# Weight tiles moved by 64 bytes inside their SBUF partition

## The chip, the cores and the metric

The kernel runs on one core of a Trainium2 chip. The metric is the device time of one execution in microseconds (us); the time quoted for a kernel is the median of its runs. Engines are named as in the profile: PE is TensorE's matmul side, PEld its weight loads, DVE is VectorE, ACT is ScalarE, POOL is GpSimd, SP is the engine whose queue issues the DMAs.

## The reference

The reference computes one batch of 256 tokens of width 1024 through two blocks, all in fp32.

The first block is a mixer (8 heads of causal attention with a learned decay, beside a depthwise convolution of width 31), a cross attention over 256 memory tokens, and a mixture of experts: 32 experts in 4 groups, one group and two experts of it for each token. The second block has two layers. Each is a gated feed-forward network (1024 to 2816 to 1024), a mixing part (a gated linear recurrence in layer 0, stick-breaking attention of 16 heads in layer 1) and a second feed-forward network:

```
y = (silu(t @ w_gate[e]) * (t @ w_up[e])) @ w_down[e]         # expert e, 1024 -> 512 -> 1024
x = x + 0.5 * ((silu(h @ w_g) * (h @ w_u)) @ w2)              # feed-forward, four of them
x = x + rglru(...)          # layer 0
x = x + stick_breaking(...) # layer 1
```

All weights, about 400 MB, are read once from HBM.

## The kernel before, in words

**Layout.** Activations lie with channels on the 128 partitions and the 256 tokens along the free dimension. A weight is brought in tiles of 128 partitions x 2048 fp32 values (8192 bytes of each partition, 1 MB in all).

**Three matmuls for one.** Outside the experts each fp32 product is made of three matmuls on values rounded to fp32r. `wload` (L136 to L160) brings a tile to `raw`; ACT rounds it into `wh` (L157), DVE writes the rest, `raw - wh`, into `wl` (L158). Activations are split in the same way into a high and a low part by `split`: `xgh`/`xgl` for a normed input, `hh`/`hl` for a feed-forward network's middle. `mm3` (L174) then issues, for each 128 x 128 piece of weight,

```
mm(out, w[0], x[0], start=first, stop=False)   # wh with the high part
mm(out, w[0], x[1], start=False, stop=False)   # wh with the low part
mm(out, w[1], x[0], start=False, stop=last)    # wl with the high part
```

The weight is the operand that is loaded into the array (a PEld row of the profile, 128 columns), and the activation is streamed through it (a PE row, 256 columns). The next weight load runs while the matmul before it streams. `proj2` runs 48 such matmuls over a tile into one PSUM tile, with `xgh`/`xgl` as streams; `rowproj` runs 48 over a tile of the down projection, with `hh`/`hl` (in the recurrence `yh`/`yl`, in the cross attention `cath`/`catl`) as streams. In `product` (values, keys and queries) the roles are exchanged: activations are loaded and weight tiles are streamed, 512 columns at a time.

**A feed-forward network** has 11 rounds; each runs 48 matmuls for the gate, 48 for the up projection, and, in rounds two to ten, the 48 of the down projection of the round before. So PE's order in a round is 96 matmuls with `xg` streams and 48 with `hh`/`hl` streams. The last two down projections run together at the end, 96 matmuls (528 down matmuls for each of the four networks).

**The experts** run on plain fp32 tiles, streamed straight from where the DMA put them (L941, L967). A ring of 16 places holds them: the 8 buffers of `raw`, 3 of `wh`, 3 of `wl`, and the two tiles `xgh` and `xgl`, which are free in that stage. SP issues the next load (L171) when PE has used a place's old content.

**Memory.** Pools lie one behind the other in each partition, tiles in the order of their first use, each rounded up to 32 bytes: constants first, then `weights` (`raw`, `wh`, `wl`), then `temps` (small work tiles; the last of them is `nr16`, 6 buffers of 64 bytes), then `xgh` and `xgl`, then the pools of the stages. Where a tile begins, in bytes past a multiple of 128:

| tile | role outside the experts | before |
|---|---|---|
| `raw`, `wh`, `wl` | weights | 32 |
| `xgh`, `xgl`; `yh`, `yl` of the recurrence; `catl`; the mixer's four | streams | 64 |
| `hh`, `hl`; `xkvh`, `xkvl` | streams | 96 |
| `cath` of the cross attention | stream | 32 |
| `oh`, `oT` of the experts' routing | streams | 0 |
| `tokh`, `tokl` (tokens, loaded as weights by L846) | loaded | 96 |

Pieces of a tile begin a multiple of 512 bytes (weights) or 1024 bytes (streams) behind its start, so all pieces of a tile have the tile's own offset. `rsqrt` makes four work tiles of the tag `nr{n}`; with `n` = 16 it is called from `head_norm` alone, with one more tile of that tag live, and `after_moe` holds one such tile earlier on.

Of the kernel before, what the change touches and what calls it, by code (L numbers as in the profile page):

```python
# [10 lines left out]
I32 = mybir.dt.int32  # L11
# [5 lines left out]
P = 128  # L17
T = 256
D = 1024
KC = D // P  # L20
# [22 lines left out]
def bc(ap, shape, at):  # L43

    return ap.unsqueeze(at).to_broadcast(shape)


class Block:
    def __init__(s, ctx, tc, io):
        s.tc, s.nc, s.ctx, s.io = tc, tc.nc, ctx, io  # L50
        s.n = s.turn = s.place = 0
        s.queue = None
        pool = lambda name, bufs, **k: ctx.enter_context(tc.tile_pool(name=name, bufs=bufs, **k))
        s.cp = pool("const", 1)
        s.wp = pool("weights", 3)
        s.tp = pool("temps", 2)
        s.xp = pool("x", 1)
        s.pa = pool("acc", 1, space=PSUM)
        s.pp = pool("ps", 2, space=PSUM)
# [165 lines left out]
    def rsqrt(s, x, n):  # L225

        nc = s.nc
        xh = s.tmp([P, n], f"nr{n}", 6 if n > 4 else 8)
        nc.vector.tensor_scalar_mul(xh, x, -0.5)
        yi = s.tmp([P, n], f"nr{n}", 6 if n > 4 else 8).bitcast(I32)  # L230
        nc.vector.tensor_single_scalar(yi, x.bitcast(I32), 1, op=ALU.arith_shift_right)
        y = s.tmp([P, n], f"nr{n}", 6 if n > 4 else 8)
        nc.vector.tensor_scalar(y.bitcast(I32), yi, -1.0, float(0x5F3759DF), op0=ALU.mult, op1=ALU.add)
        u = s.tmp([P, n], f"nr{n}", 6 if n > 4 else 8)
        for _ in range(3):
            if n == 2:
                for i in range(n):
                    c = slice(i, i + 1)
                    nc.vector.scalar_tensor_tensor(u[:, c], y[:, c], xh[:, c], y[:, c], op0=ALU.mult, op1=ALU.mult)
            else:  # L240
                nc.vector.tensor_mul(u, y, y)
                nc.vector.tensor_mul(u, u, xh)
            nc.vector.scalar_tensor_tensor(y, u, 1.5, y, op0=ALU.add, op1=ALU.mult)
        return y
# [61 lines left out]
    def rows(s, st, n=D, tag="acc3"):  # L306


        got = {}

        def rows(what):
            if not got:
                got["pb"], a = s.bank(tag)
                got["x"], got["y"] = s.rstd(s.colsum(st, a[:, 0:2]), n)
            if what not in got:
                got[what] = s.spread(got["y"], got["pb"])
            return got[what]
        return rows
# [705 lines left out]
    def after_moe(s, acc, p2):  # L1024


        nc = s.nc
        gg = s.new(p2, [P, KC], "gg")
        nc.vector.tensor_mul(gg, s.col("final_g", 0, 8), s.col("ffn1_norm_2", 0, 8))

        g2 = s.tmp([P, 2 * KC], "nr16", 6).rearrange("p (k n) -> p k n", n=2)
        nc.vector.memset(g2, 1.0)
        nc.vector.tensor_mul(g2[:, :, 1], s.col("final_g", 0, 8), s.col("final_g", 0, 8))
        xg = s.pair(s.xp, KC, "xg")
        st = s.sums_pe(g2)
        for b in range(4):
            s.update(acc[b], b, 1.0, xg, gg, st)
        got = {}

        def rows(what):  # L1040
            if not got:


                x = s.tmp([P, 4], "nr4", 8)
                pb = s.bank()[0]
                nc.vector.tensor_scalar_mul(x.rearrange("p (n h) -> p n h", h=2), st["pe"].rearrange("p h n -> p n h"), 1.0 / D)
                nc.vector.tensor_scalar_add(x[:, 0:2], x[:, 0:2], EPS)
                nc.vector.scalar_tensor_tensor(x[:, 2:4], x[:, 0:2], EPS, x[:, 2:4], op0=ALU.mult, op1=ALU.add)
                y = s.rsqrt(x, 4)
                got["r"] = s.spread(y[:, 2:4], pb)  # L1050
                got["r1"] = s.spread(y[:, 0:2], pb, s.tmp([P, T]))
            return got[what]

        def rescale():
            for k in range(KC):
                nc.vector.scalar_tensor_tensor(s.xT[:, k], s.xT[:, k], s.col("final_g", k), rows("r1"), op0=ALU.mult, op1=ALU.mult)
        return xg, rows, rescale
# [124 lines left out]
    def head_norm(s, dst, ps, rows):  # L1182


        nc = s.nc
        n = 8
        m = s.tmp([P, 2 * n], f"nr{2 * n}", 6)
        for h in range(2):
            q = s.tmp([P, 512], "gs", 2)
            nc.scalar.activation(q, ps[h], AF.Square)  # L1190
            nc.scalar.copy(dst[:, h], ps[h])
            nc.vector.reduce_sum(m[:, h * n:(h + 1) * n], q.rearrange("p (a d) -> p a d", d=64), axis=AX.X)
        e = s.tmp([P, 2], "nr2", 8)
        nc.vector.tensor_scalar_mul(e, rows("x"), EPS)
        for h in range(2):
            mh = m[:, h * n:(h + 1) * n]
            nc.vector.tensor_scalar(mh, mh, 1.0 / 64, e[:, h:h + 1], op0=ALU.mult, op1=ALU.add)
        r = s.rsqrt(m, 2 * n)
        for h in range(2):
            v = dst[:, h].rearrange("p (a d) -> p a d", d=64)  # L1200
            nc.vector.tensor_mul(v, v, bc(r[:, h * n:(h + 1) * n], [P, n, 64], 2))
# [200 lines left out]
```

## Time and profile before

| | us |
|---|---|
| median of 3 runs | 1717.57 (1716.57 to 1721.44) |
| profiled execution, its own time | 1718.19 |
| its span, first to last instruction | 1716.4 |
| PE busy in the span | 1659.7 (97%) |
| DVE, ACT busy | 922.9 (54%), 704.0 (41%) |
| mean granted TensorE clock | 0.984 of full speed |

A PE row's own length overlaps with the next (matmuls are pipelined), so it is no measure of what a matmul costs. What it costs is the distance between the starts of two that follow one another; over a run of matmuls, the distance between the first start and the start behind the last, divided by their number.

### The profile page before, as it was taken

To read this page: it belongs to the slowest core of one execution; us is meant where nothing else is said; L and a number is where in the kernel's file an instruction comes from. 1 tells how busy PE (TensorE), PEld (TensorE's weight loads), DVE (VectorE), ACT (ScalarE), POOL (GpSimd) and SP (SyncE) were. 2 spreads that over 40 slices of the span, in tenths; PEclk is the share of its full clock that TensorE was granted. 3 is DMA by queue.
4 is the path that set the end of the run, shared out by engine and by line. 5 is a ranking of instruction groups with operands and counts; after the bars stand their busy time and mean duration, and the time that the engine had idled before them with its cause. 6 is when DMAs were issued, how large, how long until landed. Compare 5 with 4: busy or idle time off the path is not lost.

```text
span 1716.4 us, 28131 instructions
## 1 busy us (share of the span) xinstructions
PE 1659.7 (97%) x11883; PEld 1349.5 (79%) x11883; DVE 922.9 (54%) x1618; ACT 704.0 (41%) x1138; POOL 5.0 (0%) x19
## 2 busy tenths in 40 slices
PE   8999989999999998699999999999999999999998
PEld 7878984444444443299999999999899997689998
DVE  7998741111111110265657886556755558876554
ACT  8526532111111111244445754445644446764442
POOL 0000000000000000000000000000000000000000
PEclk9999989999999999889999999999999999899999
DMA  9334359999999999845553555554555454044530
GB/s 367 132 120 175 142 226 367 419 419 420 419 419 419 420 419 420 361 183 191 197 184 136 197 221 172 197 184 161 198 196 197 174 195 172 25 148 172 197 123 26
DMA packets 60227, 408.03 MB, mean 238 GB/s; under 512 B 6592, under 2 KB 9920, under 8 KB 11456
## 3 DMA queue, kind: packets, MB, share of 16 engines
q1 hardware_dynamic: 60096, 406.18, 61.4%
q8 instruction: 95, 1.56, 0.4%
q14 instruction: 36, 0.29, 0.0%
HBM read 405.11 MB, written 1.05 MB: 237 GB/s over the span
## 4 chain that ended last, share of the span: by engine, by line
PE 54%; DVE 2%; ACT 1%; issue 1%; DMA 0%; SPq 0%; ACTq 0%; DVEq 0%
PE A L179 6%; PE A L178 6%; PE A L177 6%; PE acc L177 5%; PE acc L178 5%; PE B L177 5%; PE B L178 5%; PE acc L179 5%; PE B L179 5%; ACT wh L157 1%; PE A L1262 1%; DVE wl L158 1%; PE A L967 1%; PE B L416 0%; PE B L408 0%
## 5 line engine op out<-in xcount | busy, mean ns | idle before, releaser
L157 ACT CAST wh<-raw 128x1024 fp32r<-128x1024 f32 (+2 forms) x378 | 378.0, 1034 | 445.0 <-issue 363.8
L158 DVE TENSOR_TENSOR wl<-raw,wh 128x1024 fp32r<-128x1024 f32 (+2 forms) x378 | 448.6, 1204 | 160.5 <-ACT wh L157 159.7
L177 PE MATMUL B<-xgh,wh 128*128 128x256 f32 x872 | 246.1, 282 | 6.9 <-ACT wh L157 6.9
L177 PE MATMUL A<-xgh,wh 128*128 128x256 f32 (+1 forms) x872 | 246.7, 283 | 0.0
L179 PE MATMUL A<-xgh,wl 128*128 128x256 f32 (+1 forms) x872 | 245.5, 282 | 0.1
L178 PE MATMUL A<-xgl,wh 128*128 128x256 f32 (+1 forms) x872 | 245.5, 282 | 0.1
L179 PE MATMUL B<-xgh,wl 128*128 128x256 f32 x872 | 245.6, 282 | 0.0
L178 PE MATMUL B<-xgl,wh 128*128 128x256 f32 x872 | 245.2, 281 | 0.0
L178 PE MATMUL acc<-hl,wh 128*128 128x256 f32 x704 | 194.7, 278 | 0.2
L179 PE MATMUL acc<-hh,wl 128*128 128x256 f32 x704 | 194.5, 277 | 0.0
L177 PE MATMUL acc<-hh,wh 128*128 128x256 f32 x704 | 193.1, 278 | 0.5 <-ACT hh L218 0.5
L177 PEld LDWEIGHTS B<-xgh,wh 128*128 128x128 f32 x872 | 164.5, 189 | 7.9 <-ACT wh L157 7.2
L179 PEld LDWEIGHTS B<-xgh,wl 128*128 128x128 f32 x872 | 164.4, 189 | 1.5 <-DVE wl L158 1.0
L178 PEld LDWEIGHTS A<-xgl,wh 128*128 128x128 f32 (+1 forms) x872 | 164.7, 189 | 0.6 <-DVE xgl L222 0.4
L177 PEld LDWEIGHTS A<-xgh,wh 128*128 128x128 f32 (+1 forms) x872 | 164.8, 189 | 0.3
L179 PEld LDWEIGHTS A<-xgh,wl 128*128 128x128 f32 (+1 forms) x872 | 164.7, 189 | 0.4 <-DVE wl L158 0.3
L178 PEld LDWEIGHTS B<-xgl,wh 128*128 128x128 f32 x872 | 164.7, 189 | 0.5 <-DVE xgl L222 0.2
L852 DVE COPY gx<-B 128x128 f32<-128x128 f32 x64 | 18.6, 291 | 231.9 <-PE B L846 223.6
L941 PE MATMUL A<-raw,gx 128*64 128x512 f32 x560 | 130.1, 603 | 8.6 <-DMA raw<-in_w_gu_dram 6.2
L178 PEld LDWEIGHTS acc<-hl,wh 128*128 128x128 f32 x704 | 132.1, 188 | 0.6 <-DVE hl L219 0.6
L179 PEld LDWEIGHTS acc<-hh,wl 128*128 128x128 f32 x704 | 132.2, 188 | 0.0
L177 PEld LDWEIGHTS acc<-hh,wh 128*128 128x128 f32 x704 | 130.9, 188 | 1.2 <-ACT hh L218 1.1
(407 smaller groups left out, 2422.4 us busy)
## 6 DMA issues: line engine op xcount, KB each, us to landing
raw<-in_ffn_w_dram SPq DMA_DIRECT2D x132, 1024.0 KB, 4.8
raw<-in_w_gu_dram SPq DMA_DIRECT2D x70, 1024.0 KB, 19.9
raw<-in_w_down_dram SPq DMA_DIRECT2D x34, 1024.0 KB, 19.9
wh<-in_w_gu_dram SPq DMA_DIRECT2D x22, 1024.0 KB, 19.9
wl<-in_w_gu_dram SPq DMA_DIRECT2D x22, 1024.0 KB, 19.9
wh<-in_w_down_dram SPq DMA_DIRECT2D x11, 1024.0 KB, 19.9
wl<-in_w_down_dram SPq DMA_DIRECT2D x11, 1024.0 KB, 19.9
raw<-in_a_w_in_dram SPq DMA_DIRECT2D x8, 1024.0 KB, 5.0
```

Of the source, the lines that this page charges most:

```text
L157: nc.scalar.copy(wh[:, lo:hi], raw[:, lo:hi])
L158: nc.vector.tensor_sub(wl[:, lo:hi], raw[:, lo:hi], wh[:, lo:hi].bitcast(F32))
L177: mm(out, w[0], x[0], start=first, stop=False)
L178: mm(out, w[0], x[1], start=False, stop=False)
L179: mm(out, w[1], x[0], start=False, stop=last)
L852: nc.vector.tensor_copy(dst, pg[:, :, i])
L941: s.pe(s.nc.tensor.matmul(ps[g * CAP:(g + 1) * CAP], gx[t // 2][:, 2 * (t % 2) + c], w[:, g, c * 512:c * 512 + 512], start=t + c == 0, sto ...
L967: s.pe(nc.tensor.matmul(pd[n * CAP:(n + 1) * CAP], hx[:, 2 * t + c], w[:, c, n * 512:n * 512 + 512], start=t + c == 0, stop=t + c == 2))
L1262: mm(sc[:, lo:lo + ke], qT[b:b + 64, c, qb * P:qb * P + P], kT[b:b + 64, c, 0:ke], start=True, stop=True)
```

## The change

A tile `pad` of 64 bytes is put in front of the weights pool, so `raw`, `wh` and `wl` begin 64 bytes later: 96 instead of 32 bytes past a multiple of 128. The tag `nr16` at the end of `temps` gets 5 buffers instead of 6, which takes 64 bytes off again, so everything from `xgh` on stays where it is. The work tiles between (`ssq`, `sq`, `dg`, `rbc`, `tmp` and smaller ones) move by 64 bytes with the weights. No instruction is added, removed or put elsewhere.

```
         s.wp = pool("weights", 3)
+        s.new(s.wp, [P, 16], "pad", bufs=1)
         s.tp = pool("temps", 2)
...
     def rsqrt(s, x, n):
-        xh = s.tmp([P, n], f"nr{n}", 6 if n > 4 else 8)
+        xh = s.tmp([P, n], f"nr{n}", 5 if n > 8 else 6 if n > 4 else 8)
...
-        yi = s.tmp([P, n], f"nr{n}", 6 if n > 4 else 8).bitcast(I32)
+        yi = s.tmp([P, n], f"nr{n}", 5 if n > 8 else 6 if n > 4 else 8).bitcast(I32)
...
-        g2 = s.tmp([P, 2 * KC], "nr16", 6).rearrange("p (k n) -> p k n", n=2)
+        g2 = s.tmp([P, 2 * KC], "nr16", 5).rearrange("p (k n) -> p k n", n=2)
...
-        m = s.tmp([P, 2 * n], f"nr{2 * n}", 6)
+        m = s.tmp([P, 2 * n], f"nr{2 * n}", 5)
```

(`y` and `u` of `rsqrt` are changed like `xh`.)

## Rows read from the trace of the kernel before

**Rows 1.** The page: busy time by engine, and PE in 40 slices of the span.

```profile
PE 1659.7 (97%) x11883; PEld 1349.5 (79%) x11883; DVE 922.9 (54%) x1618; ACT 704.0 (41%) x1138; POOL 5.0 (0%) x19
...
PE   8999989999999998699999999999999999999998
```

**Rows 2.** Windows by stage: stretch, length, busy per engine, clock, DMA share, GB/s.

```profile
260.00:735.00 475.00, 446.36 (x2555) 197.51 (x2554) 77.82 (x183) 88.89 (x204) 0.12 (x1) 0.98 0.99 409
...
1011.00:1195.00 184.00, 183.59 (x1578) 182.99 (x1577) 114.81 (x139) 82.78 (x103) 0.00 (x0) 1.00 0.53 189
...
1527.00:1716.40 189.40, 184.61 (x1567) 183.66 (x1566) 109.73 (x133) 75.80 (x91) 0.00 (x0) 1.00 0.38 134
```

**Rows 3.** Groups by line and form: instruction, count | busy us, mean ns | idle before.

```profile
L177 PE MATMUL A<-xgh,wh 128*128 128x256 f32 x864 | 244.4, 283 | 0.0
...
L177 PE MATMUL acc<-hh,wh 128*128 128x256 f32 x704 | 193.1, 278 | 0.5 <-ACT hh L218 0.5
```

**Rows 4.** Timeline of PE, layer 0's second feed-forward network: start, length, instruction.

```profile
1151.27 0.28 PE L177 MATMUL acc<-hh,wh 128*128 128x256 f32 x1
...
1156.71 0.28 PE L177 MATMUL A<-xgh,wh 128*128 128x256 f32 x1
...
1167.92 0.28 PE L177 MATMUL acc<-hh,wh 128*128 128x256 f32 x1
```

**Rows 5.** Timeline of PE, first feed-forward network, third round's 96 matmuls and what follows.

```profile
771.24 0.28 PE L177 MATMUL A<-xgh,wh 128*128 128x256 f32 x1
...
782.76 0.28 PE L177 MATMUL acc<-hh,wh 128*128 128x256 f32 x1
```

**Rows 6.** Timeline of PE, last feed-forward network, one down projection and what follows.

```profile
1565.42 0.28 PE L177 MATMUL acc<-hh,wh 128*128 128x256 f32 x1
...
1571.08 0.28 PE L177 MATMUL A<-xgh,wh 128*128 128x256 f32 x1
```

**Rows 7.** Timeline of PE, output projections of cross attention (46 steps) and recurrence (43).

```profile
217.05 0.28 PE L178 MATMUL acc<-catl,wh 128*128 128x256 f32 x1
...
222.57 0.28 PE L179 MATMUL acc<-cath,wl 128*128 128x256 f32 x1
...
987.67 0.28 PE L178 MATMUL acc<-yl,wh 128*128 128x256 f32 x1
...
992.77 0.28 PE L179 MATMUL acc<-yh,wl 128*128 128x256 f32 x1
```

**Rows 8.** Timeline of PE, gathering tokens for an expert: six matmuls.

```profile
305.34 0.40 PE L846 MATMUL B<-oh,tokl 128*128 128x256 f32 x2
...
306.04 0.22 PE L859 MATMUL B<-idr,oh 128*128 128x128 f32 x1
```

**Rows 9.** Timeline of PE, the value projection with weights as streams: 33 steps.

```profile
1234.10 0.39 PE L177 MATMUL B<-wh,xkvh 128*128 128x512 f32 x1
...
1241.80 0.39 PE L177 MATMUL A<-wh,xkvh 128*128 128x512 f32 x1
```

**Rows 10.** Timeline of SP's queue in the expert stage: issues of weight loads.

```profile
402.74 0.33 SPq L171 DMA_DIRECT2D wl<-in_w_gu_dram  x1
405.22 0.33 SPq L171 DMA_DIRECT2D xgh<-in_w_gu_dram  x1
407.73 0.33 SPq L171 DMA_DIRECT2D xgl<-in_w_gu_dram  x1
410.21 2.83 SPq L171 DMA_DIRECT2D raw<-in_w_down_dram  x2
```

**Rows 11.** Groups by line and form: the weights' splitting and the streams'.

```profile
L158 DVE TENSOR_TENSOR wl<-raw,wh 128x1024 fp32r<-128x1024 f32 x368 | 442.5, 1220 | 156.0 <-ACT wh L157 155.2 <-PE B L178 0.7
L157 ACT CAST wh<-raw 128x1024 fp32r<-128x1024 f32 x368 | 372.6, 1047 | 440.0 <-issue 360.1 <-DMA raw<-in_ffn_w_dram 22.1 <-PE A L178 21.0
...
L219 DVE TENSOR_TENSOR hl<-us,hh 128x512 fp32r<-128x512 f32 x44 | 30.4, 691 | 1.4 <-ACT hh L218 1.4
...
L218 ACT CAST hh<-us 128x512 fp32r<-128x512 f32 x44 | 27.1, 617 | 10.0 <-DVE us L1076 10.0
```

More of the change, by code (lines that the diff above doesn't have):

```diff
@@ L227, in rsqrt @@
         nc = s.nc
-        xh = s.tmp([P, n], f"nr{n}", 6 if n > 4 else 8)
+        xh = s.tmp([P, n], f"nr{n}", 5 if n > 8 else 6 if n > 4 else 8)
         nc.vector.tensor_scalar_mul(xh, x, -0.5)
-        yi = s.tmp([P, n], f"nr{n}", 6 if n > 4 else 8).bitcast(I32)
+        yi = s.tmp([P, n], f"nr{n}", 5 if n > 8 else 6 if n > 4 else 8).bitcast(I32)
         nc.vector.tensor_single_scalar(yi, x.bitcast(I32), 1, op=ALU.arith_shift_right)
-        y = s.tmp([P, n], f"nr{n}", 6 if n > 4 else 8)
+        y = s.tmp([P, n], f"nr{n}", 5 if n > 8 else 6 if n > 4 else 8)
         nc.vector.tensor_scalar(y.bitcast(I32), yi, -1.0, float(0x5F3759DF), op0=ALU.mult, op1=ALU.add)
-        u = s.tmp([P, n], f"nr{n}", 6 if n > 4 else 8)
+        u = s.tmp([P, n], f"nr{n}", 5 if n > 8 else 6 if n > 4 else 8)
         for _ in range(3):
```

## The prediction, made before the changed kernel was run

> **What bounds the kernel now.** I read the busy times first, then the stages, then the spacing of PE's matmuls inside a stage. PE is busy 97% of the span, and all 40 slices but one stand at 8 or 9 tenths [rows 1]; the change adds no instruction, so it can act only through what one instruction or one DMA costs. The stages differ in what sets their pace [rows 2]. From 260 to 735 us, in the experts, the DMA engines are busy 0.99 of the time at 409 GB/s and PE's weight loads only 197.5 of 475 us: this stage goes at the pace of the transfers. In a feed-forward network (1011 to 1195 us) PE is busy 183.59 of 184.00 us at full clock while DVE has 114.81, ACT 82.78 and the DMA share is 0.53: PE's matmuls bound it, and nothing is hidden behind anything else there. A tenth of a per cent in the spacing of these matmuls is a tenth of a per cent of the stage.
>
> How many they are: the `xg` streams have six groups like the first of rows 3 (three matmuls, tiles A and B), 6 x 864 = 5,184; the `hh`/`hl` streams three like the second, 3 x 704 = 2,112.
>
> What one costs is not constant, and this is the row to look at. Streams `xg`: 96 matmuls from 1156.71 to 1167.92, 116.8 ns each. Just ahead of them, 48 with `hh`/`hl`: 1151.27 to 1156.71, 113.3 ns each [rows 4]. Same form, same weight buffers, same granted clock. But the same `xg` streams ran at 120.0 ns in one round (771.24 to 782.76, 96 matmuls) [rows 5], and the same `hh`/`hl` at 117.9 ns in the last network (1565.42 to 1571.08, 48) [rows 6]. So a run of matmuls settles into one of several rhythms: 113.3, 116.8, 117.9 or 120.0 ns, and holds it for a whole tile. Where the weights lie against the streams is a candidate for what picks the rhythm, and it is what the change moves.
>
> Counting the down projections in the timeline, 24 runs of 48 (eight in each of the first three networks) are like the one in rows 4, 1,152 matmuls; the other 960 (first runs, tails, all of the last network) are like rows 6. Of the 96-long `xg` runs two are like rows 5.
>
> **The change part by part.**
>
> *The streams against the weights.* The weights begin 96 instead of 32 bytes past a multiple of 128. Weights minus streams, modulo 128: for `xg`, `yh` and the mixer from 96 to 32; for `hh`/`hl` and `xkvh` from 64 to 0; for `cath` from 0 to 64, `catl` from 96 to 32. What rows tell of these distances:
> - 96: `xg` 116.8 or 120.0 [rows 4, 5]; `yh`/`yl` (5.10 us in 43 steps) 118.6 [rows 7]; tokens loaded from 96 with a stream at 0, (306.04 - 305.34)/6 = 116.7 [rows 8].
> - 64: 113.3 or 117.9 [rows 4, 6].
> - 0 mixed with 96: `cath`/`catl` (5.52 us in 46 steps) 120.0 [rows 7].
> - 32 with 256 columns: no row. With 512 columns and the roles exchanged, weights as streams: 7.70 us in 33 steps, 233.3 ns, twice 116.7 [rows 9].
>
> So 116.7 to 116.8 is what most pairs of offsets come to, whatever they are, and 113.3 is seen with `hh`/`hl` at a distance of 64 alone. I take from that: the `xg` runs keep 116.8 (0 us), and the `hh`/`hl` runs, at a distance of 0, lose the 113.3 rhythm and come to the common 116.8. Their sum: 1,152 x (116.8 - 113.3) = +4.0 us; 960 x (116.8 - 117.9) = -1.1 us; together +2.9 us. Nothing lies beside it: PE is the bound of these stages [rows 2].
>
> Both ends, from the extremes of the rows. `xg`: 5,184 x (113.3 - 116.8) = -18.1 us to 5,184 x (120.0 - 116.8) = +16.6 us. `hh`/`hl`: all at 113.3, 960 x -4.6 = -4.4 us; all at 120.0, 1,152 x 6.7 + 960 x 2.1 = +9.7 us. I stay near the middle because 116.8 is the row nearest to most of the work.
>
> *The small projections* (recurrence, cross attention, mixer, stick-breaking; some 770 matmuls of the same form) keep their mean, 0 us; from 118.6 to 113.3 or 120.0 they give -4 to +1 us. *The 512-column products*, weights as streams (nine of 48, 432 matmuls), 0 us; at twice the extreme rhythms, 226.6 or 240.0 instead of 233.3, they give -2.9 or +2.9 us.
>
> The Trainium skill, "SBUF — State Buffer", section "Who interferes with whom", says that PE has two SBUF read ports of its own, one for the streamed operand and one for weight loads, independent of each other, and that PE waits on nobody. By that rule the address of the weights could not change a stream's spacing at all and the sum would be 0 instead of +2.9 us; the trace neither needs nor refutes it, but the rule does not explain four rhythms of one form at one clock [rows 4 to 6].
>
> *The transfers.* All 14 `raw`, `wh`, `wl` places of the experts' ring now begin at 96. The trace has places at two offsets: issues follow one another by 2.48 us (402.74 to 405.22, after `wl` at 32), 2.51 (`xgh` at 64) and 2.48 (`xgl` at 64, to 410.21) [rows 10]. SP issues when PE has freed a place, and PE follows the landings at a DMA share of 0.99, so that is the pace of the loads. No difference by offset, 0 us; by the scatter of these rows, 0.02 us for each of 192 loads, -3.8 to +3.8 us.
>
> *DVE and ACT.* Splitting: 1,024 elements take 1220 ns on DVE with weights at 32, 512 take 691 with `hl` at 96; ACT 1047 and 617 [rows 11]. The difference is 529 and 430 ns for 512 more elements, so a fixed part of 162 and 187 ns is left at either offset: no sign of a dependence, 0 us. Had it one, PE's idle time in the network is under 0.5 us of 184 [rows 2], and DVE has a third of that stage free.
>
> *Five buffers for `nr16`.* `head_norm` holds five tiles of it at once (`m` and the four of `rsqrt`), and all their writers and readers are on DVE in program order; a buffer that comes round one tile earlier waits for nothing. 0 us. The moved work tiles of `temps` keep their form: 0 us.
>
> Sum: 1718.19 us of the profiled execution + 2.9 = 1721.1; the median of the runs shown lies 0.6 us below the profiled one, so 1720.5 us. That is 0.17% above the median before. About 0.3% (5.2 us) is what a measurement of this kernel can tell from no change.
>
> **The rivals.**
>
> *Nothing moves.* In one spacing a stream of 256 columns passes and a weight load of 128 [rows 3], so 128 bytes of stream go by in the time of 64 bytes of weights; if what sets the rhythm repeats every 128 bytes of the stream, the shift is a whole period and every rhythm stays. For it: 116.7 at so many offsets [rows 4, 8, 9]. Against it: that would not say why `hh`/`hl` alone reach 113.3. Time: 1717.6. The same would be seen if the tiles did not move as the change says.
>
> *Faster: `xg` finds the 113.3 rhythm.* It exists for the same code at a full tile's length [rows 4], and `xg` has 5,184 matmuls. Fully: 1717.6 - 18.1 = 1699.5; with the loss of `hh`/`hl`, 1702.4; with half of the `xg` runs, about 1709. Against it: no run of `xg` has it now.
>
> *Slower: `xg` leaves 116.8 for a worse one.* At 117.9 in all runs it is 5,184 x 1.1 = +5.7 us, with `hh`/`hl` +8.6: 1726.2. At the 120.0 of rows 5, +16.6 and with `hh`/`hl` 1737. For it: `xg` already has two such runs, and `yh`, at `xg`'s offset and distance, stands at 118.6 [rows 7]. It decides from a mean of `xg` above 117.3 ns (5,184 x 0.5 = 2.6 us, with the 2.9 of `hh`/`hl` above 5.2).
>
> *Slower: the loads.* If a load's time hangs on its offset by the whole scatter of rows 10, 192 x 0.02 = +3.8 us on top of the forecast, 1724.3. The Trainium skill, "DMA: Bandwidth & Descriptors", section "How a descriptor splits into AXI transactions", says that a transaction starts at a multiple of 256 bytes and that what a descriptor leaves over costs further beats of 32 bytes. If it held for the SBUF side, a packet of 8192 bytes that starts at 96 instead of 32 would need two beats more in some 257, an estimate by that page of 0.8% of the loads' time; rows 10, with `xgh` and `xgl` at 64, show no step of that kind.
>
> **How the numbers follow.** `hh`/`hl` lose their rhythm and little else happens: 0.26. Nothing moves: 0.16. These two make "within 0.3%", 0.42. Faster by more: 0.29. Slower by more: `xg` worse 0.24, loads 0.05, together 0.29. The likeliest case has 1716 to 1724 as its own range. The range of 8 in 10 reaches to 1702 (below it lies the case that nearly all `xg` runs reach 113.3, 0.1) and to 1731 (above it, most `xg` runs near 120.0, 0.09).
>
> **What would show it.** In the timeline of PE, the down projections of the first three networks at about 116.8 instead of 113.3 ns a matmul, the `xg` runs still at 116.8, and the last network's down projections at 116.8 or 117.9. The expert stage as long as before, with issues 2.49 us apart. DVE and ACT groups of rows 11 unchanged to a few ns. The forecast is wrong if `xg` runs have another rhythm, or if the `hh`/`hl` runs keep 113.3 at a distance of 0; it is wrong in its ground if the rhythms change without regard to the offsets.

## The result: 1732.6 us, slower, and the profile after

The changed kernel takes 1732.62 us (median of four runs, 1732.44 to 1734.38), the kernel before 1717.76 us beside it (1716.57 to 1721.44). The ratio is 1.0081, interval 1.0064 to 1.0099: slower by 0.8%. The forecast was 1720.5 us, within 0.3%, with a range up to 1731; the time lies above the range.

The page's line of busy times, to be held against [rows 1]: same instructions, PE 15.3 us busier, the other engines as before.

```profile
PE 1675.0 (97%) x11883; PEld 1368.5 (79%) x11883; DVE 922.7 (53%) x1618; ACT 704.1 (41%) x1138; POOL 5.0 (0%) x19
```

Windows of the same stages (columns as in [rows 2]; the second and third are shifted to where these networks now lie). The experts are as fast as before, 411 GB/s at a DMA share of 0.99. In the second, 1,568 matmuls take 186.62 us of PE where there were 1,578 in 183.59, at the same clock of 1.00.

```profile
260.00:735.00 475.00, 445.65 (x2565) 199.21 (x2564) 77.89 (x183) 89.24 (x204) 0.12 (x1) 0.98 0.99 411
1015.20:1202.00 186.80, 186.62 (x1568) 186.01 (x1567) 113.35 (x137) 82.17 (x100) 0.00 (x0) 1.00 0.52 186
```

Groups by line and form, to be held against [rows 3] and [rows 11]: matmuls with `xgh` at 285 ns instead of 283, with `hh` at 283 instead of 278; DVE and ACT to the nanosecond what they were.

```profile
L178 PE MATMUL A<-xgh,wh 128*128 128x256 f32 x864 | 246.3, 285 | 0.0
...
L178 PE MATMUL acc<-hh,wh 128*128 128x256 f32 x704 | 196.5, 283 | 0.1
...
L159 DVE TENSOR_TENSOR wl<-raw,wh 128x1024 fp32r<-128x1024 f32 x368 | 442.3, 1220 | 165.8 <-ACT wh L158 164.8 <-PE B L179 0.7
...
L158 ACT CAST wh<-raw 128x1024 fp32r<-128x1024 f32 x368 | 372.5, 1047 | 457.4 <-issue 372.9 <-PE A L179 22.6 <-DMA raw<-in_ffn_w_dram 22.4
```

The timeline of PE, same network as [rows 4], and the value projection that answers to [rows 9]:

```profile
1159.07 0.28 PE L178 MATMUL acc<-hh,wh 128*128 128x256 f32 x1
...
1164.82 0.28 PE L178 MATMUL A<-xgh,wh 128*128 128x256 f32 x1
...
1176.18 0.28 PE L178 MATMUL acc<-hh,wh 128*128 128x256 f32 x1
...
1241.11 0.39 PE L180 MATMUL B<-wh,xkvl 128*128 128x512 f32 x1
...
1246.55 0.39 PE L180 MATMUL A<-wh,xkvl 128*128 128x512 f32 x1
```

48 matmuls with `hh`/`hl` from 1159.07 to 1164.82: 119.8 ns each (before 113.3). 96 with `xg` from 1164.82 to 1176.18: 118.3 (before 116.8). 24 products of 512 columns from 1241.11 to 1246.55: 226.7 (before 233.3). Means over the whole profile, counted from start to start inside the runs of matmuls (before, after):

```
xg             116.91  118.28 ns   5,184 x +1.37 = +7.1 us
hh/hl          115.15  119.73      2,112 x +4.58 = +9.7 us
512 columns    233.09  230.57        432 x -2.52 = -1.1 us
```

Together +15.7 us, with some tenths more for the small projections (`yh` 118.7 to 119.9); the spans differ by 14.3. Of these, 13.8 us arise between the first and the last `hh`/`hl` matmul of the four networks (3.7, 4.0, 3.7 and 2.4 us by the starts in the two traces). The remainder, under 2 us, is not attributed: the experts were 2.2 us shorter in this execution (471.5 us from their first matmul to their last, before 473.7), and in the small stages PE also waits for others.

### The profile page after: what moved, and what is told of

Read it like the earlier page. It is cut to its first block, busy times and chain, and to the rows that moved or that the text cites. A ratio compares the mean times of both kernels' runs of the same rounds, so it can differ in the third digit from the quotient of the medians.

```text
span 1730.7 us, 28131 instructions
## 1 busy us (share of the span) xinstructions
PE 1675.0 (97%) x11883; PEld 1368.5 (79%) x11883; DVE 922.7 (53%) x1618; ACT 704.1 (41%) x1138; POOL 5.0 (0%) x19
## 4 chain that ended last, share of the span: by engine, by line
PE 55%; DVE 2%; ACT 1%; DMA 0%; issue 0%; SPq 0%; ACTq 0%; DVEq 0%
PE acc L178 6%; PE acc L179 6%; PE acc L180 6%; PE B L179 6%; PE B L178 6%; PE A L178 6%; PE A L180 6%; PE B L180 6%; PE A L179 6%; PE A L1263 1%; DVE wl L159 1%; PE A L968 0%; PE B L417 0%; PE B L409 0%; PE A L186 0%; PE B L186 0%
## 5 line engine op out<-in xcount | busy, mean ns | idle before, releaser
L179 PE MATMUL acc<-hl,wh 128*128 128x256 f32 x704 | 198.4, 283 | 0.1
L180 PE MATMUL acc<-hh,wl 128*128 128x256 f32 x704 | 198.1, 283 | 0.0
```

## Experiments

Theories. *Distance*: what counts is weights minus streams, modulo some power of two. *Own offset*: where the weights lie, whatever the streams. *Pair*: both, but not by their difference. *Side effect*: the five buffers, or the moved work tiles. Each ratio is against the kernel before, timed beside the run on the same chip (medians 1719.5 to 1721.4). Sweeps, which run groups of matmuls and nothing else, are shown in outline; of edits the telling lines are shown.

### The cost by itself

```
order = [(w, x) for w in (0, 32, 64, 96) for x in (0, 32, 64, 96)]
for w, x in order + order[::-1]:    # two groups of 48 each
    sweep(weights[w // 4:], streams[x // 4:])
```

> The disputed cost by itself: nothing of the block is computed, only the groups of 48 matmuls of 256 columns that a projection makes (high x high, high x low, low x high over eight chunks), back to back, two groups for each of 16 pairs of offsets (weights at 0, 32, 64, 96 and streams at 0, 32, 64, 96 bytes past a multiple of 128), in one order and then in the opposite one. Distance theory (only weights minus streams, modulo 128, counts): four values along the diagonals, distance 96 near 116.9 ns, 64 near 115.2, 32 near 118.3, 0 near 119.7, the numbers of the kernels before and after. Own-offset theory (the weights' place alone counts): one value for each weights' offset whatever the streams', 32 at 115 to 117, 96 at 118.3 to 119.7. Pair theory (both places count, and not by their difference): sixteen values without either pattern. Neither place counts and it is something else of the changed kernel: one value everywhere.

Measured, ns from start to start behind the first 24 matmuls of a pair; first order / opposite order (the first pair, which begins at some 215 ns a matmul, is left out):

```
           stream 0        32              64              96
weights 0  -/117.8         116.8/116.7     117.8/117.8     118.9/118.9
       32  118.3/118.3     117.8/117.8     118.9/116.7     117.8/117.8
       64  121.0/120.7     118.3/118.3     117.8/117.8     118.9/116.7
       96  118.9/118.6     120.9/120.7     118.3/118.3     117.8/117.8
```

The values run along diagonals: distance 0 has 117.8 four times, distance 32 has 118.3 (118.9 where it wraps around). That is against the own-offset theory and against "one value". The sizes were not all as expected: 64 has 117.8 or 120.8, by whether it wraps, so the period is longer than 128. And the same pair at distance 96 had 116.7 in one order and 118.9 in the other: what ran before has a part in it. (Here the two weight tiles, and the two stream tiles, differ by 128 modulo 256; in the kernel each two agree. The next sweep has that right.)

### Side effects alone, and all distances kept

```
-        xh = s.tmp([P, n], f"nr{n}", 6 if n > 4 else 8)
+        xh = s.tmp([P, n], f"nr{n}", 5 if n > 8 else 6 if n > 4 else 8)
...
+        s.new(s.tp, [P, 16], "padt", bufs=1)
```

> Side effects alone: nr16 has five buffers and the work tiles of temps lie 64 bytes further, weights and streams stay where they were. If the place of the weights is the cause, 1717.6 us, xg at 116.9 ns a matmul and hh/hl at 115.2, as before. If the five buffers or the moved work tiles are the cause, 1732.6 us, xg at 118.3 and hh/hl at 119.7.

1719.37 us, 0.9996 [0.9984, 1.0008]; `xg` 116.87 ns, `hh`/`hl` 114.20. So neither the buffers nor the work tiles are the cause. The mean of `hh`/`hl`, expected at 115.2, counts how many networks reach 113.3 in the profiled execution: all four here, three in the kernel before, two in the next run (116.25).

```
+        s.new(s.wp, [P, 8], "padw", bufs=1)
```

> Weights, work tiles and streams all lie 32 bytes further, so that every distance is that of the kernel before, and every offset is new (weights 64, xg 96, hh/hl 0). Distance theory: 1717.6 us, xg 116.9 ns, hh/hl 115.2. Own-offset and pair theories: no reason for these numbers; by the weights' offset halfway between before and after some 1725 us, xg 117.6, hh/hl 117.4.

1717.97 us, 0.9990 [0.9980, 1.0000]; `xg` 116.88, `hh`/`hl` 116.25. Every offset is new, the distances are the old ones, and so is the time.

### The streams moved instead of the weights

```
-        xh = s.tmp([P, n], f"nr{n}", 6 if n > 4 else 8)
+        xh = s.tmp([P, n], f"nr{n}", 5 if n > 8 else 6 if n > 4 else 8)
```

(and so for each `nr16`; no pad)

> The weights stay at 32; nr16 has five buffers and nothing makes up for it, so that all streams lie 64 bytes lower (xg 0, hh/hl 32). The distances are those of the kernel after. Distance theory: 1732.6 us, xg 118.3 ns, hh/hl 119.7. Own-offset theory: 1717.6 us, xg 116.9, hh/hl 115.2. Pair theory: neither, anywhere from 113.3 to 120.0 ns, 1699 to 1744 us.

1733.95 us, 1.0075 [1.0052, 1.0098]. Timeline of PE, the same network:

```profile
1149.49 0.28 PE L177 MATMUL A<-xgh,wh 128*128 128x256 f32 x1
...
1160.85 0.28 PE L177 MATMUL acc<-hh,wh 128*128 128x256 f32 x1
...
1166.60 0.28 PE L177 MATMUL A<-xgh,wh 128*128 128x256 f32 x1
```

96 `xg` in 11.36 us are 118.3 ns, 48 `hh`/`hl` in 5.75 are 119.8; the means are 118.27 and 119.73, the 512-column products 230.57: the numbers of the kernel after, with the weights where they were before. The distance theory had this to 0.1 ns. The own-offset theory is out, and after two pairs of kernels with the same distances at other offsets so is the pair theory.

### Finer, and a third distance in the kernel

```
for d in tuple(range(0, 256, 16)) + (288, 320, 448, 480):
    for i in range(2):
        up(weights[d // 4:], streams)      # 96 matmuls
        down(weights[d // 4:], streams)    # 48 matmuls
```

> The cost by itself, finer: nothing of the block is computed. Streams at 0 modulo 512 all along; weights 0 to 240 bytes further in steps of 16, then 288, 320, 448 and 480. At each distance the pattern of an up projection (groups u, 48 matmuls) and that of a down projection (groups d, 48 matmuls), twice, in one order and then in the opposite one. Distance theory with a period of 128: 0, 32, 64, 96 give what 128, 160, 192, 224 give; u at 32 (and 160, 288) 118.3 ns, at 96 (and 224, 480) 116.7 or 118.9; d at 64 (and 192, 320, 448) 113.3 or 117.8, at 0 and 128 119.7. A longer period: 64 and 192 differ, as in the first sweep 120.7 and 117.8. If the place counts in steps of 32 bytes, 16 gives what 0 or 32 gives; if it counts by the byte, it lies between or apart.

Timeline of PE in this sweep (`u01d64`: up projection, second time, distance 64; `d` for the down projection):

```profile
44.84 0.28 PE L177 MATMUL d01d0r<-X,W 128*128 128x256 f32 x1
...
50.60 0.28 PE L177 MATMUL u00d16r<-X,W 128*128 128x256 f32 x1
...
101.73 0.28 PE L177 MATMUL u01d32r<-X,W 128*128 128x256 f32 x1
...
113.09 0.28 PE L177 MATMUL d01d32r<-X,W 128*128 128x256 f32 x1
...
169.01 0.28 PE L177 MATMUL u01d64r<-X,W 128*128 128x256 f32 x1
...
179.89 0.28 PE L177 MATMUL d01d64r<-X,W 128*128 128x256 f32 x1
...
442.05 0.28 PE L177 MATMUL u01d192r<-X,W 128*128 128x256 f32 x1
...
453.35 0.28 PE L177 MATMUL d01d192r<-X,W 128*128 128x256 f32 x1
```

Distance 0: 48 in 5.76 us, 120.0 ns. Distance 32: 96 in 11.36, 118.3. Distance 64: 96 in 10.88, 113.3. Distance 192: 96 in 11.30, 117.7. Up and down pattern agree within 0.3 ns at every distance and time (the first groups at distance 0, which do not run back to back, left out). The whole list (up; first order / opposite order where they differ by over 0.2):

```
  0 120.0          64 113.3         128 120.0/118.6   192 117.8          288 118.3
 16 118.3          80 118.8/118.7   144 118.3/120.0   208 116.7          320 113.3
 32 118.4          96 117.3/118.7   160 119.9/120.0   224 116.7          448 113.3
 48 117.8         112 120.0         176 118.1         240 120.0/117.3    480 116.7
```

Modulo 512 the kernel before has `xg` at 480 and `hh`/`hl` at 192, the kernel after 32 and 256 (which the sweep lacks; its 0 is the same modulo 256). By the list that is 116.7, 117.8 (with 113.3 as a second rhythm at 448, which is 192 modulo 256), 118.3 and 120.0; the means of the profiles are 116.9, 115.2 (groups of 113.3 and of 117.8), 118.3 and 119.7. A period of 128 is out: 32 has 118.4 and 160 has 120.0, 80 has 118.7 or more and 208 has 116.7, in both orders. Steps of 16 count.

The recurrence's `yh`/`yl`, at which no experiment aimed, are a test of the list. Counted through the pools they go from 96 before to 160 after, modulo 512, and from 118.7 to 119.9 ns; they are at 128 in the next kernel, with 118.7, and at 224 in the one with the parameters' tile moved (further below), with 116.7. The list has all four numbers.

```
+        s.new(s.wp, [P, 8], "padw", bufs=1)
+        s.new(s.xp, [P, 8], "padx")
```

(and five buffers for `nr16`)

> Weights at 64 instead of 32, streams where they were before: distances 0 for xg, 96 for hh/hl. Distance theory with the numbers of the first sweep: xg 117.8 ns, 5,184 x 0.9 = +4.7 us; hh/hl at the distance that xg had, 116.7 to 118.9, 2,112 x 1.5 to 3.7 = +3 to +8 us; together 1725 to 1730 us. Own-offset theory: halfway, 1725 us, with xg at 117.6. If only a distance of 32 or a shift by 64 hurts: 1717.6 us.

1736.66 us, 1.0082 [1.0063, 1.0100]; `xg` 119.91, `hh`/`hl` 117.77. Distance 0 gives `xg` the 120.0 of the second sweep; the 117.8 of the first one, by which I had expected 1725 to 1730, I put down to its tile bases, which no run shows. `hh`/`hl` at 224 have 117.8, not the sweep's 116.7; the last sweep below has 117.9 there too, and two first groups of this kernel have 116.7, so 224 also has two rhythms.

### The two parts of the change by themselves

`hh`/`hl` and `xkv` alone:

```
-        gg = s.new(p2, [P, KC], "gg")
+        gg = s.new(s.tp, [P, KC], "gg", bufs=1)
...
-        x = s.tmp([P, 2], "nr2", 8)
+        x = s.tmp([P, 2], "nr2", 7)
...
-                x = s.tmp([P, 4], "nr4", 8)
+                x = s.tmp([P, 4], "nr4", 7)
```

> One part alone: weights and xg where they were before, hh/hl and xkv 64 bytes lower, so that their distances are those of the kernel after (0 modulo 256). Distance theory: hh/hl 119.7 ns, 2,112 x 4.6 = +9.7 us, xg 116.7 or a little above, the 512-column products -1 us: 1726 to 1728 us. If the weights' own offset did it: 1717.6 us.

1730.81 us, 1.0066 [1.0052, 1.0081].

```profile
1162.90 0.28 PE L177 MATMUL A<-xgh,wh 128*128 128x256 f32 x1
...
1174.21 0.28 PE L177 MATMUL acc<-hh,wh 128*128 128x256 f32 x1
...
1179.97 0.28 PE L177 MATMUL A<-xgh,wh 128*128 128x256 f32 x1
...
1260.99 0.28 PE L178 MATMUL A<-xgl,wh 128*128 128x256 f32 x1
...
1272.08 0.28 PE L177 MATMUL acc<-hh,wh 128*128 128x256 f32 x1
...
1277.82 0.28 PE L177 MATMUL A<-xgh,wh 128*128 128x256 f32 x1
...
1289.13 0.28 PE L177 MATMUL acc<-hh,wh 128*128 128x256 f32 x1
```

`hh`/`hl` take 5.76 us for 48, 120.0 ns, as expected. But `xg`, which nobody moved, has 11.31 us for 96, 117.8 ns in all four networks, and 116.7 in most groups outside them. That is 3 to 5 us more than expected. The last four rows show where it changes, in the third network: 95 `xg` matmuls ahead of the first `hh`/`hl` take 11.09 us, 116.7 ns, and 96 behind it 11.31, 117.8; it is so in all four networks.

`xg` alone: the kernel of the streams moved, with a pad ahead of `hh`:

```
+            s.new(p2, [P, 16], "pad")
```

> The other part alone: xg (and the first stage's streams) 64 bytes lower, weights and hh/hl where they were before, so that xg has the distance of the kernel after (32) and hh/hl that of before (192). Distance theory: xg 118.3 ns, 5,184 x 1.4 = +7.1 us, hh/hl 115.2: 1725 us. If hh/hl came to 113.3 only by way of an xg group at 120.0, which is gone here, hh/hl at 117.8 throughout, another 2,112 x 2.6 = +5.6 us: 1730 us.

1731.39 us, 1.0065 [1.0051, 1.0080].

```profile
1164.52 0.28 PE L177 MATMUL A<-xgh,wh 128*128 128x256 f32 x1
...
1175.87 0.28 PE L177 MATMUL acc<-hh,wh 128*128 128x256 f32 x1
...
1181.52 0.28 PE L177 MATMUL A<-xgh,wh 128*128 128x256 f32 x1
```

`xg` is at 118.2 ns; `hh`/`hl`, which nobody moved, are at 117.7, and no group of them is at 113.3: the second alternative of the expectation. Each part alone costs 0.65%, both together 0.81%: the parts do not add up, because a group's rhythm also hangs on the group before it. That the way to 113.3 leads over an `xg` group at 120.0 is not shown: in the kernel before two networks of three went that way [rows 5], the third did not.

### Modulo 256, and a kernel faster than both

```
-        s.par = s.cp.tile([P, NPAR], F32, name="par")
+        s.par = s.new(s.tp, [P, NPAR], "par", bufs=1)
```

> Weights 1,408 bytes lower (the parameters' tile is put behind them), all else in place: modulo 128 every offset is that of the kernel before, modulo 256 the weights' distances change by 128 (xg 96 instead of 224, hh/hl 64 instead of 192). Period of 128: 1717.6 to 1720 us, as before. Period of 256, with the second sweep's numbers: hh/hl at 113.3 throughout (-3.9 us), xg at 117.4 to 118.7 (+2.6 to +9.3 us): 1716 to 1725 us, told apart by the spacing rather than by the time.

1719.64 us, 0.9999 [0.9989, 1.0009]: the time decides nothing, the spacing does. Timeline of PE, the second and the third network:

```profile
1159.74 0.28 PE L177 MATMUL A<-xgh,wh 128*128 128x256 f32 x1
...
1171.00 0.28 PE L177 MATMUL acc<-hh,wh 128*128 128x256 f32 x1
...
1342.78 0.28 PE L177 MATMUL A<-xgh,wh 128*128 128x256 f32 x1
...
1354.17 0.28 PE L177 MATMUL acc<-hh,wh 128*128 128x256 f32 x1
```

96 `xg` take 11.26 us, 117.3 ns, and 11.39 us, 118.7 ns. But for first and last groups, `xg` is at 117.3 in three of the four networks and at 118.7 in the third, never at its 116.7; `hh`/`hl` at 113.7 where `xg` is at 117.3, at 117.8 where it is at 118.7. With the offsets modulo 128 all unchanged, a period of 128 is out in the kernel too.

```
-        gg = s.new(p2, [P, KC], "gg")
+        gg = s.new(s.tp, [P, KC], "gg", bufs=1)
...
-        x = s.tmp([P, 2], "nr2", 8)
+        x = s.tmp([P, 2], "nr2", 6)
...
-        m = s.tmp([P, 2 * n], f"nr{2 * n}", 6)
+        m = s.tmp([P, 2 * n], f"nr{2 * n}", 5)
```

> All streams of the projections are put where the second sweep had 113.3 ns: xg 192 and hh/hl 64 bytes on from where they were in their 256 (224 both), weights at 32, so that weights minus streams is 64 modulo 256 for both (five buffers for nr16, six for nr2, gg among the work tiles; nothing else). Distance theory with a period of 256: xg and hh/hl at 113.3 ns throughout, 5,184 x -3.6 = -18.7 us and 2,112 x -1.85 = -3.9 us: 1695 to 1697 us, faster than both kernels. Rival, that the rhythm is only a matter of what PE did before and the sweep's 113.3 is not reached between other engines' work: xg at 117.8, some 1722 us.

(Modulo 256 that is 160 bytes on for `xg` and 128 for `hh`/`hl`, not the 192 and 64 of the expectation; the 224 is right, and modulo 512 the distances are 64 and 320.) 1706.97 us (1700.85 to 1713.62), 0.9934 [0.9919, 0.9949]: faster than both. Timeline of the profiled run (1700.85 us):

```profile
1150.73 0.28 PE L177 MATMUL A<-xgh,wh 128*128 128x256 f32 x1
...
1161.61 0.28 PE L177 MATMUL acc<-hh,wh 128*128 128x256 f32 x1
...
1167.05 0.28 PE L177 MATMUL A<-xgh,wh 128*128 128x256 f32 x1
```

96 `xg` in 10.88 us, 48 `hh`/`hl` in 5.44: 113.3 ns both, and so in every network but for its first and last groups. Outside the networks most groups are at 117.8, so the mean of `xg` is 114.16. The median is 10 us above what was expected. Once more, for its profile:

> The kernel with all streams at the distance 64 once more, for its profile: its six times lay between 1700.85 and 1713.62 us, and the profiled one, 1700.85, had all four feed-forward networks at 113.3 ns. A network has 1,056 xg and 528 hh/hl matmuls, so one that settles at 117.8 instead costs 1,584 x 4.45 = 7.05 us. If that is the spread, this run is at 1701, 1708 or 1715 us and the profile shows none, one or two networks at 117.8 ns. If the spread is something else, the networks are at 113.3 whatever the time.

1700.41 us, and all four networks at 113.3: as the theory has it for this time, but it shows no network at 117.8.

### What picks the rhythm, and what the distance acts on

```
for n in range(30):
    for i in range(8):
        d = STEPS[(i * (2 * (n % 4) + 1) + n) % 8]
        start(d, n)      # 48 matmuls into one bank, then ACT copies 8 + 8n columns of it
```

> The cost by itself, after pauses: nothing of the block is computed. Groups of 48 matmuls in the pattern of an up projection, each kept waiting by a ScalarE copy of the tile before (8 to 240 columns, so that the start falls at 30 different moments), at the distances 0, 32, 64, 192, 224, 320, 448 and 480 of weights to streams, in four different orders. If a distance has one rhythm, all 30 groups of it have one mean (32: 118.3 ns, 0: 120.0). If a distance has two and the start picks one, groups of 64, 192, 320 and 448 are divided between 113.3 and 117.8, and groups of 224 and 480 between 116.7 and 120.0. If one of the four distances with 113.3 has that rhythm alone, it would be the place to put the streams.

Groups of 30 at each rhythm: distance 64, 14 at 113.3 and 16 at 117.8; 320, 26 and 4; 192 and 448, all at 117.8; 224 and 480, all at 116.7; 32, all at 118.2 to 118.5; 0, all at 120.0 but the first. So, other than expected, 192 and 448 are not divided here, nor 224 and 480. Two starts of distance 64, both behind a group of distance 32, timeline of PE:

```profile
255.42 0.28 PE L177 MATMUL q4d64r<-X,W 128*128 128x256 f32 x1
...
258.25 0.28 PE L177 MATMUL q4d64r<-X,W 128*128 128x256 f32 x1
...
430.52 0.28 PE L177 MATMUL q8d64r<-X,W 128*128 128x256 f32 x1
...
433.24 0.28 PE L177 MATMUL q8d64r<-X,W 128*128 128x256 f32 x1
```

24 matmuls in 2.83 us, 117.9 ns, and in 2.72, 113.3: same addresses, same predecessor, a pause of another length. Behind 32 the rhythm alternated with every four steps of the pause from the second on, and so it did behind 480, 320 and 192; that points to the moment of the start and away from chance. The sweeps had 113.3 at 448 in an unbroken stream and 117.8 after a pause: both rhythms hold there too.

```
for m in (128, 64, 32):                    # weight columns
    for d in (0, 32, 64, 96, 128, 192, 224, 320):
        up(weights[d // 4:], streams, m)   # 48 matmuls
```

> What the distance acts on: groups of 48 matmuls in the pattern of an up projection, nothing of the block computed, with 128, 64 and 32 columns of weights instead of 128 alone, streams of 256 columns as ever, at the distances 0, 32, 64, 96, 128, 192, 224 and 320, three times. If it is the reading of the weights for the next matmul that gets in the way of the stream's reading (or the other way round), fewer weight columns get in the way less: with 32 the distances come together, within 1 ns, at or below 113.3. If the distance acts on something that doesn't scale with the weights read, the table of 128 columns (120.0, 118.3, 113.3 or 117.8, 116.7) is there at 64 and 32 columns too.

Spacing in ns by distance, third time through and behind the first 24 matmuls, and the weight loads (minimum, median, maximum ns in the rows of a tile):

```
columns    0      32     64     96     128    192    224    320
  128    120.0  118.4  117.7  117.4  118.9  117.7  117.9  113.4
   64    113.4  116.7  119.0  116.6  116.8  116.7  119.0  119.0
   32    113.4  117.3  113.4  113.4  113.4  113.4  117.4  113.4
```

```profile
L177 PEld LDWEIGHTS m128d0n1r<-X,W x16: 188/192/192, 150.6 to 156.0; 128*128 128x128 f32 x16
...
L177 PEld LDWEIGHTS m128d320n1r<-X,W x16: 187/188/188, 190.3 to 195.4; 128*128 128x128 f32 x16
...
L177 PEld LDWEIGHTS m64d0n1r<-X,W x16: 134/134/134, 195.8 to 200.9; 128*64 128x64 f32 x16
...
L177 PEld LDWEIGHTS m32d0n1r<-X,W x16: 107/108/108, 240.7 to 245.8; 128*32 128x32 f32 x16
```

The stream is the same in all rows. The number of weight columns read beside it differs, and with it the rows of the result in PSUM, which this sweep does not separate. So the table hangs on more than the stream: with 32 columns six of eight distances are at 113.4, with 128 one, and the load itself takes 192 ns at distance 0 where it takes 188 at 320. My expectation ("within 1 ns") missed two distances, 32 and 224, which stay at 117.3 and 117.4; and with 64 columns the distances do not come together at all (113.4 to 119.0).

The parameters' tile behind the weights as above, `gg` back in its place, and a pad ahead of `hh`:

```
-        nm, sm = s.tmp([P, n], f"nm{n}", 4), s.tmp([P, n], f"sm{n}", 4)
+        nm, sm = s.tmp([P, n], f"nm{n}", 3), s.tmp([P, n], f"sm{n}", 3)
...
+            s.new(p2, [P, 56], "pad")
```

> All streams at the distance 320 modulo 512 (in the sweep of starts 26 of 30 groups at 113.3, against 14 of 30 at 64). The parameters' tile lies behind the weights, which moves these by 128 modulo 512; softmax's three small work tiles have three buffers instead of four, and a pad of 224 bytes stands ahead of hh/hl. Theory of the two rhythms that the start picks from: more networks, and the single projections between them, settle at 113.3, so the six times come together near 1698 to 1702 us, where those at 64 had a median of 1706.97. If the distance counts modulo 256 alone, 320 is the same as 64: a median near 1707 and a spread of 10 us again.

1704.49 us (1701.95 to 1712.77), 0.9903 [0.9887, 0.9920]: above the 1698 to 1702 expected, with a spread of 10.8 us. The profiled run is the longest, 1712.77 us, and it shows one cause of the spread. Timeline of PE, the second and the third network:

```profile
1161.66 0.28 PE L177 MATMUL A<-xgh,wh 128*128 128x256 f32 x1
...
1172.97 0.28 PE L177 MATMUL acc<-hh,wh 128*128 128x256 f32 x1
...
1178.62 0.28 PE L177 MATMUL A<-xgh,wh 128*128 128x256 f32 x1
...
1357.36 0.28 PE L177 MATMUL A<-xgh,wh 128*128 128x256 f32 x1
...
1368.24 0.28 PE L177 MATMUL acc<-hh,wh 128*128 128x256 f32 x1
...
1373.68 0.28 PE L177 MATMUL A<-xgh,wh 128*128 128x256 f32 x1
```

96 `xg` take 11.31 us (117.8 ns) in the second network and 10.88 (113.3) in the third, in one execution. The first is like the second, the fourth like the third: two networks at 117.8, by 7.05 us each 14.1, against 11.9 between this run and the 1700.85 of the placement at 64, which had none. The intervals of this placement and of the one at 64 touch, and two of its four networks did not settle, so that 320 settles more often in the kernel is not shown.

## Why the prediction was wrong, point by point

*What bounds the kernel.* Right: PE's spacing sets the networks, and 13.8 of the 14.3 us are there. So was the reading that one form holds several rhythms.

*`xg` keeps 116.8.* This is the step that failed: "So 116.7 to 116.8 is what most pairs of offsets come to, whatever they are". The term, 0 us, measured +7.1. The rows did not carry it. Of the three, `xg` [rows 4] and the tokens with `oh` [rows 8] both lie at distance 96 modulo 128, so they are one distance seen twice; and the 512-column products [rows 9], which the list has beside distance 32, lie at 64, with the roles exchanged. There was no row at 32 with 256 columns, as the text says, and 32 has 118.2 to 118.5 in the second sweep, in the sweep of starts and in the kernel with the streams moved. Nor were `xg` and `yh` at one distance: that holds modulo 128 alone. Modulo 512 they lie at 480 and at 96, where the list has 116.7 and, as one of two, 118.7; `yh` had 118.6. The rival that `xg` leaves 116.8 for something worse, 0.24, is what happened; its point of decision, a mean above 117.3, was passed.

*`hh`/`hl` lose 113.3 and come to 116.8.* The loss is right. The place they come to is wrong by the same step: 119.7 instead of 116.8, +9.7 us instead of +2.9. The rows had a hint: `cath`/`catl`, with distance 0 among its two, at 120.0 [rows 7]. I used it only for the upper bound, which was +9.7. (A small misreading beside it: the first 21 matmuls of the double down projections at the end of three networks ran at 113.5, not at 117.9, some 0.3 us.)

*Nothing moves.* Its ground, a rhythm that repeats every 128 bytes, is refuted by the kernel with the parameters' tile moved: modulo 128 nothing differed, and `xg` went from 116.7 to 117.3 and 118.7.

*The rule of independent reads.* The Trainium skill, "SBUF — State Buffer", section "Who interferes with whom", would have made the sum 0. Here the measurements differ from it: the distance between the two operands alone moves the spacing, fewer weight columns beside the same stream move the spacing by up to 6.6 ns at distance 0 (120.0 to 113.4), and the load takes 192 ns or 188 by the distance alone.

*Loads, DVE, ACT, five buffers, 512-column products.* 411 GB/s against 409, 1220 and 1047 ns as before, the side effects alone at 0.9996: zero as forecast. The 512-column products gained 1.1 us where I had 0; the forecast's low end was -2.9.

*The range.* Each miss alone would have stayed inside it, `xg` at 1720.5 + 7.1 = 1727.6 and `hh`/`hl` at 1720.5 + 6.8 = 1727.3; both together leave it. The change moves the distance of both at once, and I had bounded them apart and let 0.09 lie above 1731.

## What to carry to other kernels

Where matmuls run back to back, take the spacing from start to start inside runs of one form, and sort it by the difference of the two operands' addresses (modulo 256 at least, 512 to be safe), not by either address: a spacing seen at one difference says nothing of another. A placement is tried cheaply by a sweep of matmuls alone, as long as it has the kernel's own tile bases and order; and a placement that reaches a fast rhythm may do so only in part of the executions, so it wants several runs and the profile of one of the longest. Moving streams and weights together by 32 bytes cost nothing here (0.9990). Moving either alone changed the spacing each time, and the time by anything from -0.7% (streams at 64) to +0.8%.

## What the runs showed of the hardware that was not expected

- At a granted clock of 1.00, a 128 x 128 x 256 matmul follows the next at 113.3 to 121.0 ns. The distance of its two SBUF operands sets which rhythms it can hold; where there are two, the start or the group before picks one. No group had a mean below 113.3, with 32 weight columns either.
- At the distances 64 and 320 the same addresses hold 113.3 or 117.8 ns, at 320 for a whole network; in the sweep of starts the moment of the start picks which. Two networks at 117.8 come to 14.1 us, and an execution of 1712.77 us had two; that this makes up the whole spread of the fastest kernels, 1700.85 to 1713.62 us, is not shown.
- The rhythm of one group reaches into the next: `xg` unmoved went from 116.7 to 117.8 ns in the networks when only `hh`/`hl` moved, and `hh`/`hl` unmoved lost 113.3 when only `xg` moved.
- Which distance is good hangs on how much is read: distance 0, the worst of eight with 128 weight columns (120.0), is the best with 64 (113.4). And 512-column products with the weights as streams ran at 226.7 ns a product at a distance of 0 modulo 256 and at 233.3 at 192 [rows 9].
- Whether the distances repeat after 256 bytes or only after 512 or more stays open: 64 and 320 agree in the second sweep (113.3), 192 and 448 differ there (117.8 and 113.3) and agree after pauses (117.8).
- What the two reads collide on inside the memory is not shown by any run here.
